# The up projection of seven products: sums of three token blocks made under the output projection, the last block's rows out of the load ring, down's first tiles moved

## The chip, the cores and the metric

The kernel runs on one core of one Trainium2 chip. Its time is the device time of one execution, in microseconds. The kernel before takes 2249.46 us (median of three runs, 2248.82 to 2249.55).

The engines of a core take their instructions in order, each from its own queue, and wait for one another by semaphores: TensorE (PE; PEld is its weight load), VectorE (DVE), ScalarE (ACT), GpSimd (POOL), and SyncE (SP), which here only issues DMA transfers.

## The reference

One layer of a streaming encoder for 1024 tokens of width 1024: two mixers, a merge, an output projection, then a gated MLP with a causal convolution of three taps. The change touches the path from the output projection on, all in float32:

```
x   = x + gate1 * (mix @ w_o)                                # 1024 x 1024
h2  = rms_norm(x, norm2_w) * (1 + scale2) + shift2
up  = h2 @ ffn_w_up                                          # 1024 x 5632
a, v = up[..., :2816], up[..., 2816:]
a   = gelu(causal_dwconv(a, ffn_conv_w, ffn_conv_b))
x   = x + gate2 * ((a * v) @ ffn_w_down)                     # 2816 x 1024
```

## The kernel before, in words

**Tiles and stages.** The tokens are 8 blocks of 128, the width of the MLP 22 tiles f of 128 columns. A float32 product is made of three passes: each operand is split into a high part (a cast on ScalarE, L143) and a low part (the rest, a subtraction on VectorE, L151), and hi x hi, hi x lo and lo x hi are summed in a PSUM bank. TensorE's matmuls come from one helper (L63), its transposes from L66; GpSimd's sums of two tiles are `gtt` (L139), its scalings `gmul` (L136).

**Output projection** (`wo`, up to L1566). For each block, four column quarters of 24 matmuls of 128 x 256 each; VectorE adds each result to the residual (L1537). `norm2` then squares a finished block (ScalarE, L1580), makes the root mean square (VectorE L1582, GpSimd L203) and scales the rows (GpSimd L136). `norm2_out` transposes the rows (tiles x2t), and ScalarE copies them out with scale and shift (L1602), the two halves of the width apart.

**Up projection in seven products** (`ups`). The matrix product of 2 x 2 blocks (token halves by halves of the width, against a and v columns) is made with seven products P1 to P7 instead of eight. Their token sides are B11, B21 (blocks 0 to 3, two halves of the width), B22 (second half of the width of blocks 4 to 7), and four combinations: T1 = f1 - B11, T2 = f2 - T1, T3 = f2 - f1, T4 = B21 - T2, where f1 and f2 are the halves of a block b of 4 to 7. Before, T1 is made in `norm2_out`; T2 is made there as a sum and split later by `late`, T3 too, and the sums of T4 (two on GpSimd for each block: L1631, and one through L139) are made by `late`, for blocks 4 to 7 in a row, when the pass "p5" begins. The weight sides are sums of the a and v columns of tile f, made by GpSimd in `prep` from raw tiles that `raw_w` loads (L1468, wa.. and wv..) into a ring "wr" of three tiles; the finished halves lie in a ring "w" of six (wP). `prep` runs LA = 5 products ahead. Each product is 12 matmuls of 128 x 512. Tiles 0 to 3 go in three passes: "pre" (P1 and P2, which need blocks 0 to 3 only), "p5" (P5), "rest" (P6, P7, P3, P4); tiles 4 to 21 go as "all" seven. After P3 ScalarE, VectorE and ScalarE make convolution and gelu of tile f (acc), after P4 GpSimd multiplies it by v (L139) and SyncE stores it (L1726).

**Down projection** (`downs`, `fetch`). 44 steps (22 tiles by two column halves), each 8 blocks of 3 matmuls. A step loads the gated tile (gr) and the weights (wdr), GpSimd scales the weights by the gate, and both are split (gh, gl, wd). Step 0 uses the rings of the up projection; the other steps use a ring of 16 tiles, laid over the memory that the combinations leave. `fetch` runs two steps ahead.

**What sets the order.** A planner (PEOrder) fixes TensorE's order: generators offer work with due times and ranks, as in `yield ((("xn", b),) + ..., 5.0)`: not before mark xn of block b plus 5 us of matmul time. The other engines take the program order as their scheduler arranges it. Memory is given out by pools: a tile laid over an older one waits until the last reader of that one is done.

Of the kernel before, what the change touches and what calls it, by code (L numbers as in the profile page):

```python
# [114 lines left out]
def _body(tc, nc, ctx, A, out):  # L115
# [1454 lines left out]
    last_sum = []  # L1570

    def norm2():
        for b in range(NB):
            yield ((("x1", b),) + ((("h2", b - 2),) if b >= 2 else ()), 0.0)
            if b < HB2 or b == NB - 1:
                xn = pw.tile([P, D], F32, tag="wr", bufs=3, name=f"xn{b}")
            else:
                xn = x_tile(f"xn{b}")
# [5 lines left out]
            gmul(xn, x1[b], rb)  # L1584
            xns[b] = xn
# [5 lines left out]
    def norm2_out():  # L1591
        for b in range(NB):
            yield ((("xn", b),) + ((("wo", 0),) if b == 0 else (("h2", b - 1),)), 7.0 if b in (0, NB - 1) else 5.0)
            xn = xns[b]
# [1 line left out]
            f = xn.rearrange("p (k c) -> p k c", c=P)
            f1, f2 = f[:, 0:4, :], f[:, 4:8, :]
            for k4 in (0, 4):
# [1 line left out]
                transposes(t, [xn[:, k * P:(k + 1) * P] for k in range(k4, k4 + 4)])  # L1600
                for k in range(k4, k4 + 4):
                    nc.scalar.activation(xn[:, k * P:(k + 1) * P], t[:, (k - k4) * P:(k - k4 + 1) * P], AF.Identity,  # L1602
# [213 lines left out]
```

## Time and profile before

| | us |
|---|---|
| median of three runs | 2249.46 |
| lowest, highest | 2248.82, 2249.55 |
| the profiled execution, its own time | 2251.65 |
| span of the profiled execution | 2249.9 |
| TensorE busy in the span (93.8%) | 2109.9 |
| VectorE, ScalarE, GpSimd busy | 1369.0, 902.5, 843.9 |

The mean granted clock of TensorE in that execution is 0.973 of full speed. A row of the timeline has a start and a duration in us, the engine, the line of the kernel, the operation with its output and inputs, the shape, how many instructions are drawn together, and in brackets the idle time of the engine ahead of it and the operation or transfer that ended it. PE rows overlap, since matmuls are pipelined.

### The profile page before, as it was taken

The page shows a single profiled execution, that of the slowest core. Times are in us where ns is not written, and L with a number is a line of the kernel's source. Part 1 is how long each engine was busy: PE and PEld are TensorE (multiplying, and loading weights), DVE is VectorE, ACT ScalarE, POOL GpSimd, SP SyncE. Part 2 cuts the span into 40 slices and gives each one's busy share as a digit, 9 for nine tenths or more (in the row PEclk, how much of TensorE's full clock was granted, in tenths as well). Part 3 has the DMA queues.
Part 4 walks back from the last instruction along what each step waited for, and adds up shares of the span by engine and source line. Part 5 has one row for each costly group of instructions (what it writes and reads, how often), then busy time and mean ns, then how long its engine had stood idle before and what let it go on. Part 6 is the DMA issues. An engine that isn't in the chain of part 4 may idle for free.

```text
span 2249.9 us, 30778 instructions
## 1 busy us (share of the span) xinstructions
PE 2109.9 (94%) x11553; PEld 1815.7 (81%) x11553; DVE 1369.0 (61%) x2197; ACT 902.5 (40%) x1817; POOL 843.9 (38%) x603
## 2 busy tenths in 40 slices
PE   7887899999999999899999999998899999999999
PEld 6776787878878799888778888897678888878887
DVE  6779499654655536658548885625665555554433
ACT  4554422363454522336225663226343343333231
POOL 4246620131122313338447760313653444442221
PEclk7999899999999999999999999999999999999999
DMA  8345742424333327588654427423232222244644
GB/s 251 104 126 161 180 130 89 131 75 136 94 94 113 94 78 231 187 267 274 231 162 122 141 76 243 131 76 94 78 110 85 85 82 79 83 141 150 215 147 153
DMA packets 279430, 309.32 MB, mean 137 GB/s; under 512 B 38815, under 2 KB 220396, under 8 KB 279024
## 3 DMA queue, kind: packets, MB, share of 16 engines
q1 hardware_dynamic: 279280, 307.35, 44.1%
q8 instruction: 91, 1.49, 0.3%
q14 instruction: 59, 0.48, 0.1%
HBM read 223.63 MB, written 83.66 MB: 137 GB/s over the span
## 4 chain that ended last, share of the span: by engine, by line
PE 36%; DVE 5%; issue 4%; POOL 4%; DMA 2%; ACT 1%; POOLq 0%; SPq 0%; ACTq 0%; DVEq 0%
PE d L63 11%; PE wo L63 4%; PE yb L63 4%; PE mx L63 3%; PE my L63 3%; PE m L63 3%; PE s L63 2%; PE mz L63 2%; PE o L63 1%; PE ya L63 1%; PE pT L66 1%; DVE qst L1186 1%; POOL acc L139 1%; DVE PTl L1258 1%; ACT P L1234 1%
## 5 line engine op out<-in xcount | busy, mean ns | idle before, releaser
L63 PE MATMUL d<-wd,gh 128*128 128x512 f32 x704 | 217.9, 391 | 2.5 <-DVE wd L151 1.8
L63 PEld LDWEIGHTS d<-wd,gh 128*128 128x128 f32 x704 | 132.8, 189 | 30.8 <-DVE wd L151 2.1
L63 PE MATMUL d<-wd,gl 128*128 128x512 f32 x352 | 137.6, 391 | 0.6 <-DVE gl L151 0.6
L139 POOL TENSOR_TENSOR wdr<-wdr,gf 128x512 f32<-128x512 f32 x44 | 61.2, 1392 | 162.9 <-DMA wdr<-in_ffn_w_down 124.9
L151 DVE TENSOR_TENSOR wd<-wdr,wd 128x512 fp32r<-128x512 f32 x44 | 31.3, 712 | 107.7 <-ACT wd L143 107.6
L143 ACT CAST wd<-wdr 128x512 fp32r<-128x512 f32 x44 | 27.3, 620 | 147.0 <-POOL wdr L139 128.7
L63 PEld LDWEIGHTS d<-wd,gl 128*128 128x128 f32 x352 | 66.5, 189 | 14.7 <-DVE gl L151 1.0
L1234 ACT ACTIVATE P<-s,nm 128x512 f32<-128x512 f32 (+2 forms) x96 | 55.3, 582 | 53.2 <-DVE nm L1232 44.1
L614 DVE TENSOR_TENSOR lt<-X 128x62 f32<-128x62 f32 (+30 forms) x62 | 68.0, 1097 | 11.0 <-DMA X<-bd_d 8.9
L136 POOL TENSOR_SCALAR P<-P,sm 128x896 f32<-128x896 f32 (+4 forms) x64 | 50.4, 794 | 63.9 <-DVE nm L1232 16.5
L139 POOL TENSOR_TENSOR acc<-acc,vv 128x512 f32<-128x512 f32 x44 | 63.8, 1469 | 24.4 <-ACT acc L1720 24.4
L63 PE MATMUL mz<-T2h,wP 128*128 128x512 f32 x176 | 62.4, 417 | 11.1 <-ACT wP L143 9.9
L151 DVE TENSOR_TENSOR gl<-gr,gh 128x1024 fp32r<-128x1024 f32 x44 | 60.6, 1377 | 15.6 <-ACT gh L143 15.3
L63 PE MATMUL m<-B21h,wP 128*128 128x512 f32 x176 | 60.1, 402 | 4.6 <-ACT u L1697 4.6
L66 PE MATMUL pT<-ident,P 128*128 128x128 f32 x288 | 48.9, 279 | 13.4 <-DVE PTl L1258 10.0
L1257 ACT CAST PTh<-pT 128x512 fp32r<-128x512 f32 (+2 forms) x96 | 46.0, 484 | 37.2 <-PE pT L66 36.9
L1116 DVE SCALAR_TENSOR_TENSOR ada<-wada,sc,ada 128x1024 f32<-128x1024 f32 x28 | 41.2, 1471 | 32.1 <-DMA wada<-in_w_ada 32.0
L63 PE MATMUL m<-B11h,wP 128*128 128x512 f32 x176 | 58.4, 395 | 0.0
L63 PE MATMUL my<-T4h,wP 128*128 128x512 f32 x176 | 57.8, 389 | 0.2 <-DVE vv L1708 0.2
L63 PE MATMUL mx<-B22h,wP 128*128 128x512 f32 x176 | 57.8, 389 | 0.0
L63 PE MATMUL my<-T3h,wP 128*128 128x512 f32 x176 | 57.8, 389 | 0.0
L63 PE MATMUL mx<-T1h,wP 128*128 128x512 f32 x176 | 57.3, 389 | 0.0
(1436 smaller groups left out, 7460.1 us busy)
## 6 DMA issues: line engine op xcount, KB each, us to landing
gr<-gg_d SPq DMA_DIRECT2D x44, 512.0 KB
wada<-in_w_ada SPq DMA_DIRECT2D x32, 512.0 KB
gg_d<-acc SPq DMA_DIRECT2D x22, 512.0 KB
wdr<-in_ffn_w_down SPq DMA_DIRECT2D x44, 256.0 KB
x<-in_x SPq DMA_DIRECT2D x16, 512.0 KB
ad<-in_w_ada SPq DMA_DIRECT2D x16, 512.0 KB
sg_d<-gst SPq DMA_DIRECT2D x32, 256.0 KB
q_d<-qst SPq DMA_DIRECT2D x48, 128.0 KB
```

The costliest lines, as they stand in the source:

```text
L63: self._pin(self.nc.tensor.matmul(out, lhsT, rhs, start=start, stop=stop, skip_group_check=more), cost)
L66: self._pin(self.nc.tensor.transpose(out=out, in_=in_, identity=ident), 0.107)
L136: return nc.gpsimd.tensor_scalar(o, i, by, 0.0, op0=ALU.mult, op1=ALU.add)
L139: nc.gpsimd.tensor_tensor(o, a, b, op=op)
L143: nc.scalar.copy(hi, src)
L151: return nc.vector.tensor_tensor(lo, src, hi.bitcast(F32), op=ALU.subtract)
L614: nc.vector.tensor_tensor(tv, X[:, 0:k, k:k + 1].broadcast_to([P, k, n]), X[:, k:k + 1, k + 1:64].broadcast_to([P, k, n]), op=ALU.mult)
L1116: nc.vector.scalar_tensor_tensor(acc, raw, sc[:, k:k + 1], acc, op0=ALU.mult, op1=ALU.add)
L1186: (gtt if LOP & (4 if n == "kst" else 8) else nc.vector.tensor_tensor)(o[r], raw[r], d[n][r].bitcast(F32), op=ALU.subtract)
L1234: nc.scalar.activation(Pt[:, kc], o, AF.Exp, bias=nm[:, 0:1], accum_out=sm[:, b:b + 1])
L1257: nc.scalar.copy(dh, tv)
L1258: nc.vector.tensor_tensor(PTl[:, k0:k0 + n, u * P:(u + 1) * P], tv, dh.bitcast(F32), op=ALU.subtract)
```

## The change

In `prep` the sum s1 = v1 + v2 is kept for the passes "pre", "p5" and "all"; "rest" takes P6's weights as v2 - (a1 - v1) in place of s1 - a1, the same value with one sum fewer. In `norm2` the square of block 7 has a ring tile of its own (sq7), and its rows go to two half tiles of another ring. `norm2_out` makes T1, T2 and T4's sums for blocks 4 to 7 on the spot and keeps them (`late` is a table now); `put_late` splits them when the pools for the combinations are open: T2 and T4 first, then T3. `fetch` moves ahead of `ups`, which loads the gate at tile 19 and calls `fetch(0)` at the last tile's P5; the tiles of the later down steps are three fixed sets of five.

```
@@ prep
-                if "s1" not in d:
-                    d["s1"] = h_tile(f"s1_{f}{kind}", ring="s").rearrange("p (k c) -> p k c", c=P)
-                    gtt(d["s1"], v1_, v2_, ALU.add)
-                    if "ra" in d:
+                if "s3" not in d:
+                    d["s3"] = v1_
+                    if kind != "rest":
+                        d["s1"] = h_tile(f"s1_{f}{kind}", ring="s").rearrange("p (k c) -> p k c", c=P)
+                        gtt(d["s1"], v1_, v2_, ALU.add)
+                    if kind != "p5":
                         gtt(v1_, a1, v1_, ALU.subtract)
             if q == "P6":
-                gtt(a1, d["s1"], a1, ALU.subtract)
+                gtt(a1, v2_, v1_, ALU.subtract)
@@ norm2
-            if b < HB2 or b == NB - 1:
+            if b < HB2:
                 xn = pw.tile([P, D], F32, tag="wr", bufs=3, name=f"xn{b}")
+            elif b < NB - 1:
+                xn = x_tile(f"xn{b}")
             else:
-                xn = x_tile(f"xn{b}")
+                xn = pw.tile([P, D], F32, tag="wr", bufs=3, name=f"sq{b}")
...
-            gmul(xn, x1[b], rb)
-            xns[b] = xn
+            if b < NB - 1:
+                gmul(xn, x1[b], rb)
+                xns[b] = [xn[:, c] for c in HS]
+            else:
+                xns[b] = [h_tile(f"xn{b}_{hf}", ring="s") for hf in range(2)]
+                for c, x in zip(HS, xns[b]):
+                    gmul(x, x1[b][:, c], rb)
@@ norm2_out
-            yield ((("xn", b),) + ((("wo", 0),) if b == 0 else (("h2", b - 1),)), 7.0 if b in (0, NB - 1) else 5.0)
+            yield ((("xn", b),), 6.0)
+            if b:
+                yield ((("h2", b - 1),), 1.0)
+            else:
+                yield ((("wo", 0),), 0.0)
...
                 gtt(t1, t1, b11l, ALU.subtract)
+                gtt(f2, f2, t1, ALU.subtract)
                 put("T1", tk, t1)
-                last_sum.append(nc.gpsimd.tensor_tensor(f2, f2, t1, op=ALU.subtract))
+                gtt(t4, b21h, f2, ALU.subtract)
+                gtt(t4, t4, b21l, ALU.add)
+                late[b] = {"T2": f2, "T3": f1, "T4": t4}
             pe.mark("h2", b)
-    def late(b, *names):
...
-        if "T4" in names:
-            b21h, b21l = [m[:, :, tk].bitcast(F32) for m in hc["B21"]]
-            follow(nc.gpsimd.tensor_tensor(f2, b21h, f2, op=ALU.subtract), last_sum[-1], True)
-            gtt(f2, f2, b21l, ALU.add)
-            put("T4", tk, f2)
@@ pools
-    t_ctx.close()
...
-    combos(pcm, "T2", "T3", "T4")
+    def put_late(names, bs):
+        for n in names:
+            for b in bs:
+                put(n, slice(b % HB2 * P, (b % HB2 + 1) * P), late[b][n])
+    combos(pool("pcm", pcm_ctx, side="right"), "T2", "T4")
+    put_late(("T2", "T4"), range(HB2, NB - 1))
+    t_ctx.close()
+    combos(pool("pcn", pcm_ctx, side="right"), "T3")
+    put_late(("T3",), range(HB2, NB - 1))
@@ fetch
+        def piece(name, dt, tag):
+            if n == 0:
+                return pw.tile([P, D], dt, tag=tag, bufs=3 if tag == "wr" else WB, name=f"{name}{n}")
+            return late_["pd"].tile([P, D], dt, tag=f"{name}{n % 3}", bufs=1, name=f"{name}{n}")
...
+        nc.sync.dma_start(gr, g_d[f])
+        nc.sync.dma_start(wr, wdn[f * P:(f + 1) * P, HS[hf]])
+        split(gh, gl, gr)
+        gtt(wr, wr, late_["gf2"][:, HS[hf]], ALU.mult)
+        follows[n] = split(dh, dl, wr)
@@ ups
-        for b in range(HB2, NB - 1):
-            late(b, "T2", "T3")
...
-                late(NB - 1, "T2", "T3")
-                for b in range(HB2, NB):
-                    late(b, "T4")
+                put_late(("T2", "T3", "T4"), [NB - 1])
...
+            if f == NF - 3 and q == "P4":
+                late_["gf2"] = x_tile("gf2")
+                nc.sync.dma_start(late_["gf2"], gate_d[5].broadcast_to([P, D]))
+            if f == NF - 1 and q == "P5":
+                fetch(0)
@@ after ups
-    gf2 = x_tile("gf2")
-    nc.sync.dma_start(gf2, gate_d[5].broadcast_to([P, D]))
-    fetch(0)
```

What becomes of the order. On TensorE, at the end of the output projection, before: the last three matmuls of block 7 (wo3_7), then the transposes of blocks 4, 5 and 6 (x2t4 to x2t6, half by half), then the first product of the up projection (m0_0).

```order
L63 MATMUL wo3_7_14545<-wo3_4h_13779,mh1_7_12944 128x256
L63 MATMUL wo3_7_14545<-wo3_4l_13780,mh1_7_12944 128x256
L63 MATMUL wo3_7_14545<-wo3_4h_13779,ml1_7_12945 128x256
L66 MATMUL x2t4_4_14580<-ident_73,xn4_14371 128x128 x4
L66 MATMUL x2t5_0_14604<-ident_73,xn5_14489 128x128 x4
L66 MATMUL x2t5_4_14613<-ident_73,xn5_14489 128x128 x4
L66 MATMUL x2t6_0_14637<-ident_73,xn6_14598 128x128 x4
L66 MATMUL x2t6_4_14646<-ident_73,xn6_14598 128x128 x4
L63 MATMUL m0_0_14690<-B11h_13513,wP1_0_14528 128x512
```

The same place after: the second half of block 6's transposes stands among the matmuls of the last quarter of block 7.

```order
L63 MATMUL wo3_7_14620<-wo3_0h_13772,mh1_0_12930 128x256
L63 MATMUL wo3_7_14620<-wo3_0l_13773,mh1_0_12930 128x256
L63 MATMUL wo3_7_14620<-wo3_0h_13772,ml1_0_12931 128x256
L66 MATMUL x2t6_4_14624<-ident_73,xn6_14510 128x128 x4
L63 MATMUL wo3_7_14620<-wo3_0h_13772,mh1_1_12932 128x256
L63 MATMUL wo3_7_14620<-wo3_0l_13773,mh1_1_12932 128x256
```

The transposes of blocks 4 to 6 (six sets of four) now stand between the matmuls of blocks 5 to 7 of the output projection, and the up projection's first product follows the last of these.

On GpSimd, where the sums for T4 stand before (xn with B21h or B21l: T4 of blocks 4 to 7; s_0rest, wv0rest, wa0rest: weights of tile 0 in the pass "rest").

```order
L1631 TENSOR_TENSOR xn_14371<-B21h,xn_14371 128x512
L1631 TENSOR_TENSOR xn_14489<-B21h,xn_14489 128x512
L1631 TENSOR_TENSOR xn_14598<-B21h,xn_14598 128x512
L139 TENSOR_TENSOR xn_14371<-xn_14371,B21l 128x512
L139 TENSOR_TENSOR s_0rest<-wv0rest 128x512
L1631 TENSOR_TENSOR xn_14631<-B21h,xn_14631 128x512
L139 TENSOR_TENSOR xn_14489<-xn_14489,B21l 128x512
L139 TENSOR_TENSOR xn_14598<-xn_14598,B21l 128x512
L139 TENSOR_TENSOR wv0rest<-wa0rest,wv0rest 128x512
L139 TENSOR_TENSOR xn_14631<-xn_14631,B21l 128x512
L139 TENSOR_TENSOR wa0rest<-s_0rest,wa0rest 128x512
L139 TENSOR_TENSOR wa0rest<-wa0rest 128x512
```

The same place after, from the scaling of block 7's rows (xn_0 and xn_1) to tile 0's weights; t_7 are block 7's T1 and T4, s_0p to s_3p the weight sums of the pass "p5".

```order
L136 TENSOR_SCALAR xn_0_14705<-x_7_14504,ss_13518 128x512
L136 TENSOR_SCALAR xn_1_14706<-x_7_14504,ss_13518 128x512
L139 TENSOR_TENSOR s_0p_14776<-wv0p_14774 128x512
L139 TENSOR_TENSOR t_7_14802<-xn_0_14705,B11h 128x512
L139 TENSOR_TENSOR t_7_14802<-t_7_14802,B11l 128x512
L139 TENSOR_TENSOR xn_1_14706<-xn_1_14706,t_7_14802 128x512
L139 TENSOR_TENSOR t_7_14803<-B21h,xn_1_14706 128x512
L139 TENSOR_TENSOR s_1p_14820<-wv1p_14818 128x512
L139 TENSOR_TENSOR s_2p_14843<-wv2p_14841 128x512
L139 TENSOR_TENSOR s_3p_14863<-wv3p_14861 128x512
L139 TENSOR_TENSOR t_7_14803<-t_7_14803,B21l 128x512
L139 TENSOR_TENSOR wv0rest<-wa0rest,wv0rest 128x512
```

Between the last norm and tile 0's weights GpSimd has one block's sums left; those of blocks 4 to 6 stand ahead of the norms of blocks 5 to 7, and the sum s_0rest is gone.

On ScalarE at the end of the up projection, before: acc_17622 and acc_17739 are the tiles f = 20 and 21, wd and gh the casts of down's first steps.

```order
L1720 ACTIVATE acc_17622<-acc_17622,v_93 128x1024
L1699 COPY xb_17647<-m_21_17648 128x512
L1717 ACTIVATE acc_17739<-xb_17647,v_92 128x1024
L143 CAST wd_17764<-wdr_17762 128x512
L143 CAST gh_17765<-gr_17763 128x1024
L1720 ACTIVATE acc_17739<-acc_17739,v_93 128x1024
L143 CAST wd_17789<-wdr_17787 128x512
L143 CAST gh_17790<-gr_17788 128x1024
```

The same place after.

```order
L1762 ACTIVATE acc_17626<-acc_17626,v_93 128x1024
L143 CAST gh_17704<-gr_17702 128x1024
L143 CAST wd_17706<-wdr_17703 128x512
L1741 COPY xb_17651<-m_21_17652 128x512
L1759 ACTIVATE acc_17755<-xb_17651,v_92 128x1024
L1762 ACTIVATE acc_17755<-acc_17755,v_93 128x1024
L143 CAST gh_17792<-gr_17790 128x1024
L143 CAST wd_17794<-wdr_17791 128x512
```

Step 0's casts have moved ahead of the last tile's convolution; step 1's come behind its gelu, as before.

## Rows read from the trace of the kernel before

**Rows 1.** Stretches: span, then each engine's busy us (instructions), clock, DMA share, GB/s.

```profile
1494.90:1544.30 49.40, 49.40 (x418) 49.40 (x417) 15.27 (x32) 24.33 (x55) 7.72 (x9) 1.00 0.26 86
1544.30:1657.90 113.60, 92.36 (x365) 71.58 (x364) 76.96 (x80) 54.20 (x101) 75.49 (x52) 0.89 0.30 88
1657.90:2001.20 343.30, 343.05 (x1513) 283.54 (x1511) 195.65 (x248) 132.28 (x195) 142.12 (x107) 1.00 0.27 85
2001.20:2012.60 11.40, 8.27 (x29) 6.16 (x29) 9.26 (x9) 5.00 (x6) 5.47 (x3) 0.85 0.65 207
2012.60:2249.90 237.30, 233.38 (x1030) 192.99 (x1028) 94.72 (x99) 65.61 (x82) 56.38 (x41) 1.00 0.52 170
```

**Rows 2.** TensorE: start, us, operation, [idle before <- what ended it].

```profile
1549.23 0.63 PE L66 MATMUL x2t<-ident,xn 128*128 128x128 f32 x4 [1.87 <-POOL ss L203]
1551.06 1.11 PE L66 MATMUL x2t<-ident,xn 128*128 128x128 f32 x4 [1.20 <-ACT xn L1602]
...
1562.45 0.80 PE L63 MATMUL m<-B21h,wP 128*128 128x512 f32 x1 [3.72 <-ACT u L1697]
...
1600.42 0.80 PE L63 MATMUL mz<-T2h,wP 128*128 128x512 f32 x1 [4.23 <-ACT wP L143]
...
1612.01 0.52 PE L63 MATMUL mz<-T2h,wP 128*128 128x512 f32 x1 [3.07 <-ACT wP L143]
...
1639.72 0.79 PE L63 MATMUL mz<-T2h,wP 128*128 128x512 f32 x1 [2.05 <-ACT wP L143]
```

**Rows 3.** The same view of SyncE's queue: weight loads as issued.

```profile
1545.33 0.38 SPq L1468 DMA_DIRECT2D wa3pre<-in_ffn_w_up  x1
1564.35 0.38 SPq L1468 DMA_DIRECT2D wv0p<-in_ffn_w_up  x1
1569.93 0.37 SPq L1468 DMA_DIRECT2D wv1p<-in_ffn_w_up  x1
...
1600.30 0.37 SPq L1468 DMA_DIRECT2D wa1rest<-in_ffn_w_up  x1
```

**Rows 4.** Waits of SyncE's queue from 1536 to 1660: total us, times, longest.

```profile
SPq L1468 <- DVE T4l L151: 18.6, 1, 18.6
```

**Rows 5.** The timeline of GpSimd (POOL).

```profile
1545.33 1.27 POOL L139 TENSOR_TENSOR t<-xn,B11h 128x512 f32<-128x512 f32 x1 [9.29 <-ACT xn L1602]
...
1549.28 1.12 POOL L136 TENSOR_SCALAR xn<-x,ss 128x1024 f32<-128x1024 f32 x1
...
1568.29 1.61 POOL L139 TENSOR_TENSOR s_0p<-wv0p 128x512 f32<-128x512 f32 x1 [4.53 <-DMA wv0p<-in_ffn_w_up]
...
1582.89 5.12 POOL L1631 TENSOR_TENSOR xn<-B21h,xn 128x512 f32<-128x512 f32 x3
...
1599.80 1.61 POOL L139 TENSOR_TENSOR wa0rest<-wa0rest 128x512 f32<-128x512 f32 x1
...
1630.67 2.54 POOL L139 TENSOR_TENSOR acc<-acc,vv 128x512 f32<-128x512 f32 x2 [4.35 <-ACT acc L1720]
```

**Rows 6.** The timeline of VectorE (DVE).

```profile
1544.46 0.42 DVE L1537 TENSOR_TENSOR x<-x,wo 128x256 f32<-128x256 f32 x1 [1.89 <-PE wo L63]
...
1552.12 1.75 DVE L1614 TENSOR_TENSOR xn<-xn 128x512 f32<-128x512 f32 x1 [1.18 <-POOL t L139]
...
1557.78 0.68 DVE L1614 TENSOR_TENSOR xn<-xn 128x512 f32<-128x512 f32 x1
...
1619.76 0.69 DVE L1714 TENSOR_TENSOR xb<-u,mx 128x512 f32<-128x512 f32 x1 [1.33 <-DMA wa3rest<-in_ffn_w_up]
```

**Rows 7.** Start of the down projection, timeline of TensorE.

```profile
2004.34 0.50 PE L63 MATMUL d<-wd,gh 128*128 128x512 f32 x1 [1.75 <-DVE wd L151]
```

**Rows 8.** The same of SyncE's queue.

```profile
2001.13 0.32 SPq L1754 DMA_DIRECT2D gr<-gg_d  x1
```

**Rows 9.** The same of ScalarE (ACT).

```profile
2003.78 1.15 ACT L1720 ACTIVATE acc<-acc,v 128x1024 f32<-128x1024 f32 x1 [1.75 <-DVE acc L1719]
...
2005.34 1.04 ACT L143 CAST gh<-gr 128x1024 fp32r<-128x1024 f32 x1
```

More of the change, by code (lines that the diff above doesn't have):

```diff
@@ L1569, in _body @@
     xns = {}
-    last_sum = []
+    late = {}
     def norm2():
@@ L1592, in norm2_out @@
         for b in range(NB):
[L1593 to L1594 removed]
+            yield ((("xn", b),), 6.0)
[3 more added lines that the diff above has]
+                yield ((("wo", 0),), 0.0)
             tk = slice(b % HB2 * P, (b % HB2 + 1) * P)
[L1596 to L1598 removed]
+            f1, f2 = [x.rearrange("p (k c) -> p k c", c=P) for x in xns[b]]
+            for k4, f in ((0, f1), (4, f2)):
                 t = bank("tp", f"x2t{b}_{k4}")
[L1600 removed]
+                transposes(t, [f[:, k, :] for k in range(4)])
                 for k in range(k4, k4 + 4):
[L1602 removed]
+                    nc.scalar.activation(f[:, k - k4, :], t[:, (k - k4) * P:(k - k4 + 1) * P], AF.Identity,
                                          bias=modc[:, 3 * KT + k:3 * KT + k + 1], scale=ab2[:, k:k + 1])
@@ L1609, in norm2_out @@
                 b11h, b11l = [m[:, :, tk].bitcast(F32) for m in hc["B11"]]
-                t1 = (h_tile(f"t1_{b}", ring="s") if b == NB - 1 else pt.tile([P, 512], F32, tag="tt", bufs=2, name=f"t1_{b}"))
-                t1 = t1.rearrange("p (k c) -> p k c", c=P)
+                b21h, b21l = [m[:, :, tk].bitcast(F32) for m in hc["B21"]]
+                if b == NB - 1:
+                    t1, t4 = [h_tile(f"t{i}_{b}", ring="s") for i in (1, 4)]
+                else:
+                    t1 = pt.tile([P, 512], F32, tag="t1", bufs=1, name=f"t1_{b}")
+                    t4 = pt.tile([P, 512], F32, tag="t4", bufs=3, name=f"t4_{b}")
+                t1, t4 = [t.rearrange("p (k c) -> p k c", c=P) for t in (t1, t4)]
                 gtt(t1, f1, b11h, ALU.subtract)
@@ L1645, in _body, with fetch @@
     pe.run(("wo", 1), ("h2", NB - 2))
-    t_ctx.close()
     wo_ctx.close()
     pcm_ctx = ctx.enter_context(ExitStack())
-    pcm = pool("pcm", pcm_ctx, side="right")
-    combos(pcm, "T2", "T3", "T4")
-    g_d = dr.tile([NF, P, S], F32, name="gg_d")
+    def put_late(names, bs):
[7 more added lines that the diff above has]
+    put_late(("T3",), range(HB2, NB - 1))
+    g_d = dr.tile([NF, P, S], F32, name="gg_d")
+    steps = [(hf, f) for hf in range(2) for f in range(NF)]
+    got = {}
+    late_ = {}
+    def fetch(n):
+        if n >= len(steps) or n in got:
+            return
+        hf, f = steps[n]
+        def piece(name, dt, tag):
+            if n == 0:
+                return pw.tile([P, D], dt, tag=tag, bufs=3 if tag == "wr" else WB, name=f"{name}{n}")
+            return late_["pd"].tile([P, D], dt, tag=f"{name}{n % 3}", bufs=1, name=f"{name}{n}")
+        gr = piece("gr", F32, "wr")
+        wr = piece("wdr", F32, "wr")[:, 0:512]
+        gh, gl = [piece(f"g{m}", F32R, "w") for m in "hl"]
+        d2 = piece("wd", F32R, "w")
+        dh, dl = d2[:, 0:512], d2[:, 512:1024]
+        nc.sync.dma_start(gr, g_d[f])
[3 more added lines that the diff above has]
+        follows[n] = split(dh, dl, wr)
+        got[n] = gh, gl, dh, dl
+    follows = {}
     def ups():
@@ L1729, in ups @@
             yield
[L1732 to L1760 removed]
     pe.add(2, ups(), True)
     pe.run(("up", NF - 1))
[L1763 to L1765 removed]
     pcm_ctx.close()
     pb_ctx.close()
[L1768 removed]
+    late_["pd"] = pd = pool("pd", side="right")
     xr = [pd.tile([P, 512], F32, name=f"xr{b}") for b in range(NB)]
```

32 lines of the change are left out of this document (removed).

## The prediction

> **What bounds the kernel now.** I began with the table of stretches [rows 1]: it cuts the last 755 us at the end of the output projection, the start of tile f = 4 of the up projection, the end of up and the first tenth of a step pair of down. Three of the five rows leave TensorE nothing to gain: it is busy for 49.40 of 49.40 us under the output projection, for 343.05 of 343.30 in f = 4 to 21, for 233.38 of 237.30 in the rest of down, each at a granted clock of 1.00. The long row also gives the pitch: 343.30 us for 1513 recorded matmuls, 0.227 us each. The other two rows are where time lies. From 1544.30 to 1657.90 TensorE stands for 113.60 - 92.36 = 21.2 us, and its clock is 0.89, so another 0.11 x 113.60 = 12.5 us go at the lower of its two levels: 33.7 us in all, and 79.9 of needed work. At the start of down it is 3.1 us idle and 0.15 x 11.40 = 1.7 at the lower clock: 4.8. So 38.5 us is all that this change can reach with what it touches; the floor is 2249.5 - 38.5 = 2211.
>
> Next, TensorE's timeline [rows 2], for where it stands: two transposes of normalised rows (1.9 and 1.2 us), a product P2 that waits for its bank (3.7 us), then P6 of f = 0, 1 and 3 (4.2, 3.1 and 2.1 us), each for ScalarE's cast of weights. From 1544.3, 7 sets of transposes at about 0.5 (an estimate from the first two rows) and the 144 matmuls of the passes "pre" and "p5" make 3.5 + 32.7 us, so P6 of f = 0 was due at 1580.5; it came at 1600.42. Thus 19.9 of the 33.7 us are lost ahead of that point and 13.8 behind it.
>
> Then the engines that TensorE waits for. SyncE's queue [rows 3] issues a weight load at 1545.33 and the next only at 1564.35, 19 us later, and wa1rest at 1600.30; its list of waits [rows 4] has 18.6 us for one T4 split: the load stood behind the last block's rows, which lay in the load ring until T4 was made of them. GpSimd [rows 5] has 75.49 of the 113.60 us full [rows 1] and takes its sums in the order in which the program asks: t1 sums at 1545, s_0p only after the load (1568.29, 3.9 us after its issue), the T4 sums from 1582.89, and f = 0's last weight sum ends at 1601.4. Under the output projection it had worked for 7.72 of 49.40 us [rows 1].
>
> **The change part by part.** *The sums moved under the output projection.* For blocks 4, 5 and 6 five GpSimd sums each (two for T1, one for T2, two for T4), 15 in all, leave the stretch with 33.7 us of loss or stand at its very beginning no more. One takes 1.27 us alone and about 1.7 beside VectorE (5.12 for three) [rows 5]: 19 to 26 us of queue. They go where GpSimd had 41.7 us free, so they fit; TensorE there has work at every moment, and that work is the cover. The transposes that they need move with them, from behind the last matmul of the output projection to between its matmuls: the stops of 1.9 and 1.2 us, which waited on the row norms, go. What they cost there the trace of before does not show; from below it is nothing; from above, block 7's norm queues behind block 6's five sums (8.7 us at 1.75) and all of it shows at TensorE. Block 6's first transposes stand some 36 matmuls of 49.40 / 418 = 0.118 us [rows 1], 4.2 us, ahead of the projection's end; with about 1.5 us for the copies out of the bank (an estimate) its sums end 3.7 to 6 us behind the end, block 7's power and scaling (1.12 us for the scaling [rows 5], 1.7 with both, an estimate) at 5.4 to 7.7, and its transposes are due 33 matmuls of up, 7.5 us, behind it. I take a stop of 1 us. VectorE's additions to the residual, 0.42 us [rows 6], now stand behind splits of up to 1.75; what waits for one is the bank of a product of 24 matmuls or 2.8 us, with a second bank to go on in, so nothing for those.
>
> *The last block's rows out of the ring.* Its square keeps a ring tile for a moment, its rows lie elsewhere. The load wv0p no longer waits for them or for the early splits: after 1545.33 it can go as soon as a tile of "pre" is split, near 1550 instead of 1564.35, and wa1rest near 1570, not 1600.30 [rows 3]. Its 18.6 us of wait [rows 4] go. What is late next: GpSimd's order. It has t1, T2 and T4 of block 7 (5 sums), four s sums and the three sums of f = 0, 12 in place of 23 from 1555 on: 12 x 1.3 to 1.75 = 16 to 21 us, from about 1554: ready at 1570 to 1575, plus a cast and a subtraction, before 1580.5.
>
> *Four weight sums fewer.* Per f = 0 to 3 the "rest" pass sums three tiles instead of four: 4 x 1.3 = 5 us of GpSimd, each in the chain ahead of P6 of its f.
>
> *What remains of the 33.7.* Ahead of P6 of f = 0: 1 us for block 7's transposes and 1.5 at the lower clock behind that stop (four transposes that took 0.63 us at 1549.23 took 1.11 at 1551.06, behind two stops [rows 2]). So 19.9 - 2.5 = 17.4 gained. Behind it: P6 of f = 1 lost 3.1 us, to a load that now starts 30 us sooner; I leave 1.5, since its sums still follow those of f = 0 on GpSimd. P6 of f = 3 lost 2.1; GpSimd takes acc of f = 0 ahead of its sums, and that waits for the gelu: from xb at 1619.76 [rows 6] to acc at 1630.67 [rows 5] are 10.9 us, a chain that the change leaves alone; I leave 2.5, plus 0.5 for f = 2 and 2 for the clock. So 13.8 - 6.5 = 7.3. Together 24.7.
>
> *Down's first tiles.* Before, the second step's load could not start until up's last matmul had read T4 (it went at 2001.13 [rows 8]), and VectorE's and ScalarE's work on step 0 came behind the last tile's convolution: TensorE stood 1.75 us for wd [rows 7]. After, the first tiles are made while up's last products run, and the load for step 1 lies over T1, whose last reader is P5, 48 matmuls or 10.9 us sooner. ScalarE's gelu (1.15 us at 2003.78) still comes ahead of the second gh cast (1.04 at 2005.34 before) [rows 9], and the first bank is read by the last products: I leave 2.0 of the 4.8 us, bounds 0 and 4.8. Gain 2.8. The gate's load moves up beside the weight loads of f = 19, where the DMA engines are 0.27 busy [rows 1]: nothing, and up to one load of 3.9 us late for a weight tile without that room.
>
> *The sum.* 24.7 + 2.8 = 27.5. The profiled execution took 2251.65 us (span 2249.9 and 1.75 around it): 2224.2 by its time. The runs' median is 2.2 us lower: 2222.
>
> *A rule weighed.* VectorE's same subtraction took 0.68 us with GpSimd free (1557.78) and 1.75 with it at work (1552.12) [rows 6]; the 1.07 more is most of one GpSimd sum. The Trainium skill (SBUF — State Buffer, "Who interferes with whom") has it that a VectorE instruction with two operands in SBUF and a GpSimd instruction that reads SBUF shut each other out for the whole instruction. By that rule, which the two rows agree with, the sums moved under the output projection also wait for VectorE's splits there; if all five sums of block 6 took 1.7 instead of 1.27, block 7's norm would be 2.1 us later, and the time 2224; with VectorE mostly away, as under the projection before (15.27 of 49.40 us [rows 1]), it stays 2222, which I keep.
>
> **The rivals.**
> *A, the stall moves into the output projection.* GpSimd's 15 sums get in the way of the norms of blocks 5, 6 and 7, the transposes that now stand between the projection's matmuls stop everything behind them, and each stop is followed by the lower clock. For it: TensorE takes its instructions in order, and the norm's own chain (square, power, scaling 1.12 us [rows 5]) is behind those sums on one queue. Against it: 41.7 us free. Price: 3 stops of 3 us and 2 us of clock for each, 15; gain 12.5, time 2237.
>
> *B, only the first wait goes.* P6 of f = 0 comes in time, but f = 1 to 3 still lack weights, since loads of 3.9 us, three sums and the acc sums share one ring and one queue; the 13.8 us behind 1600 stay. For it: P6 of f = 3 waited though no T4 sum was near. Against it: a pair's chain, three sums of 1.3 and two loads, is about 12 us and runs ahead, against 48 matmuls or 10.9 us. Gain 17.4 + 2.8 = 20.2, time 2229.
>
> *C, slower: down's three sets.* Tiles of down were a ring of 16, now three fixed sets of five, so that the cast of wd for step n+3 may not start until TensorE has read all of step n (before, the ring gave it the place of an earlier gr). Chain from there: cast 0.62, subtraction 0.69, against two steps of 24 matmuls or 10.9 us until it is wanted. It decides only if the chain, with loads and the queue ahead of it, comes to more than that: if each of 43 steps lost 0.8 us, 34 us, the time would be 2257. Against it: gh stood under the same bond before, and all of down lost 237.3 - 43 x 24 x 0.227 = 3 us.
>
> *D, nothing moves.* The sums could stand elsewhere and the stops stay as they are, 2249. Against it: the order of the built program has them between the norms.
>
> **How the numbers follow.** Forecast (gain of 22 to 33, time 2217 to 2227) 0.58; B 0.18; A 0.13; C 0.04; D 0.03; the remaining 0.04 is a gain near the full 38.5. The range goes from the floor, 2211, to just beyond A, 2239. About 0.2% or 4.5 us is what a measurement of this kernel can tell from no change: forecast, A, B and the floor are faster, 0.93; D same, 0.03; C slower, 0.04.
>
> **What will show it.** The first matmul of f = 4 should come at about 1544.3 + 79.9 + 9 = 1633 on this trace's clock in place of 1657.9, the granted clock up to there above 0.93 and the idle time under 8 us; wv0p issued before 1552 and wa1rest before 1575; no wait of SyncE for a T4 split; P6 of f = 0 before 1584. The output projection should show GpSimd at 27 to 34 us and TensorE still full; stops above 2 us there mean A. Waits for P6 of f = 1 to 3 above 3 us each mean B. At down's start the two stops should sum to under 2 us; idle time spread over all steps of down means C. A stretch as long as before means that I misread what holds GpSimd's order.

## The result, and the profile after

The changed kernel takes 2228.26 us (median of 4 runs, 2217.35 to 2231.01) against 2249.14 (4 runs, 2248.34 to 2249.55): a ratio of 0.990, 95% interval 0.9865 to 0.9932, 20.9 us by the medians. The forecast was 2222, with a range of 2211 to 2239. The profiled execution took 2231.01 us (span 2229.3).

Two traces are best compared by landmarks, since the part ahead of the output projection, whose instructions the change leaves alone, ran 2.7 us longer in this one: the projection's first matmul stands at 1450.91, before at 1448.20. From there:

| us | before | after | won | forecast |
|---|---|---|---|---|
| first matmul of the output projection to first of f = 4 | 209.73 | 188.86 | 20.9 | 24.7 |
| first of f = 4 to first of down | 344.15 | 342.90 | 1.2 | |
| first of down to the end of the span | 247.82 | 246.63 | 1.2 | 2.8 with the row above |
| start to first matmul of the projection | 1448.20 | 1450.91 | -2.7 | 0 |

The stretches of the changed kernel, with the columns of [rows 1]; the first two are the output projection, the third reaches to f = 4, the fifth is the start of down:

```profile
1450.90:1497.60 46.70, 46.70 (x391) 46.69 (x390) 17.63 (x28) 10.09 (x13) 12.75 (x9) 1.00 0.23 79
1497.60:1550.40 52.80, 51.71 (x436) 51.51 (x436) 24.08 (x40) 35.65 (x83) 24.85 (x21) 1.00 0.27 91
1550.40:1639.70 89.30, 82.50 (x346) 66.66 (x345) 62.88 (x73) 43.72 (x73) 53.75 (x37) 0.94 0.38 112
1639.70:1982.50 342.80, 342.80 (x1514) 283.63 (x1513) 198.53 (x250) 132.99 (x196) 142.48 (x107) 1.00 0.28 90
1982.50:1994.00 11.50, 9.66 (x42) 7.35 (x41) 9.28 (x7) 5.14 (x7) 7.44 (x4) 1.00 0.39 105
1994.00:2229.30 235.30, 230.93 (x1018) 190.56 (x1016) 115.46 (x99) 63.35 (x81) 62.19 (x40) 1.00 0.53 168
```

The reader sees the third row, which answers to the second of [rows 1]: 89.30 us in place of 113.60, GpSimd 53.75 us full in place of 75.49, and a clock of 0.94 in place of 0.89. TensorE still stands for 6.8 us there, and 0.06 x 89.30 = 5.4 us are lost to the lower clock. The projection now has idle time (1.1 us), GpSimd works 24.85 us under its second half, and up runs without a stop. The stops that remain, in TensorE's timeline:

```profile
1545.19 0.66 PE L66 MATMUL x2t<-ident,xn 128*128 128x128 f32 x4 [1.09 <-POOL xn L136]
...
1561.01 1.12 PE L66 MATMUL x2t<-ident,xn 128*128 128x128 f32 x4 [3.59 <-POOL xn L136]
```

```profile
1597.08 0.73 PE L63 MATMUL mz<-T2h,wP 128*128 128x512 f32 x2 [0.35 <-DVE wP L151]
...
1621.32 0.50 PE L63 MATMUL mz<-T2h,wP 128*128 128x512 f32 x1 [2.51 <-ACT wP L143]
```

The stops of [rows 2] ahead of P6 of f = 0 and of f = 1 and for the bank of P2 are gone (0.35 us are left within P6 of f = 1). A stop of 3.59 us for block 7's norm has come, with transposes at the lower clock behind it (1.12 us for four), and that for f = 3 has stayed (2.51; before 2.05). SyncE's queue, against [rows 3]:

```profile
1552.19 0.38 SPq L1468 DMA_DIRECT2D wa3pre<-in_ffn_w_up  x1
1554.07 0.38 SPq L1468 DMA_DIRECT2D wv0p<-in_ffn_w_up  x1
...
1579.08 0.37 SPq L1468 DMA_DIRECT2D wa1rest<-in_ffn_w_up  x1
1588.24 0.37 SPq L1468 DMA_DIRECT2D wv1rest<-in_ffn_w_up  x1
```

wv0p goes 1.9 us after wa3pre (before 19), and what is left of waits for a T4 split is 0.3 us; but wv1rest follows wa1rest only after 9 us. At down's start the stops of 0.75, 1.75 and 0.63 us come to 0.54, 1.30 and 0.42, the last two now in steps 1 and 2 (the third, at 1996.79, is not shown):

```profile
1984.05 0.73 PE L63 MATMUL d<-wd,gh 128*128 128x512 f32 x2 [0.54 <-DVE vv L1765]
...
1990.63 0.50 PE L63 MATMUL d<-wd,gh 128*128 128x512 f32 x1 [1.30 <-DVE wd L151]
```

### The profile page after: what moved, and what is told of

Same layout as the page of the kernel before. It is cut to its first block, busy times and chain, and to the rows that moved or that the text cites. A ratio compares the mean times of both kernels' runs of the same rounds, so it can differ in the third digit from the quotient of the medians.

```text
span 2229.3 us, 30774 instructions
## 1 busy us (share of the span) xinstructions
PE 2103.6 (94%) x11553; PEld 1814.4 (81%) x11553; DVE 1387.3 (62%) x2197; ACT 901.6 (40%) x1817; POOL 848.3 (38%) x600
## 4 chain that ended last, share of the span: by engine, by line
PE 41%; DVE 4%; DMA 2%; POOL 2%; issue 1%; ACT 1%; POOLq 0%; SPq 0%; ACTq 0%; DVEq 0%
PE d L63 11%; PE m L63 5%; PE my L63 5%; PE mx L63 5%; PE yb L63 4%; PE wo L63 4%; PE s L63 3%; PE mz L63 2%; PE o L63 1%; PE ya L63 1%; PE pT L66 1%; DVE qst L1186 1%; DVE PTl L1258 1%; ACT P L1234 1%; DVE nm L1227 1%
## 5 line engine op out<-in xcount | busy, mean ns | idle before, releaser
L139 POOL TENSOR_TENSOR wdr<-wdr,gf 128x512 f32<-128x512 f32 x44 | 68.7, 1564 | 163.5 <-DMA wdr<-in_ffn_w_down 148.1
L143 ACT CAST gh<-gr 128x1024 fp32r<-128x1024 f32 x44 | 46.1, 1050 | 153.6 <-PE d L63 153.1
L151 DVE TENSOR_TENSOR wd<-wdr,wd 128x512 fp32r<-128x512 f32 x44 | 61.2, 1392 | 1.2 <-ACT wd L143 1.2
```

What stands on the lines that cost most here:

```text
L139: nc.gpsimd.tensor_tensor(o, a, b, op=op)
L143: nc.scalar.copy(hi, src)
L151: return nc.vector.tensor_tensor(lo, src, hi.bitcast(F32), op=ALU.subtract)
```

## The experiments

The time of one execution spreads by more than some of these effects, so each kernel is also read by the stretch from the projection's first matmul to the first of f = 4 in its profile, called the stretch below. The changed kernel run twice gave 188.86 and 189.22 there, before and before with down's edits 209.73 and 209.84: in these two pairs it repeats to 0.4 us. Inside it less is fixed: P6 of f = 0 came 139.8 us after the projection's start in the first profile of the changed kernel and 138.5 in the second. Each stretch is read from one profile; each ratio is to the kernel before in the same batch, whose median lay between 2249.14 and 2252.13.

| kernel | stretch, us | median, us | ratio to before (95%) |
|---|---|---|---|
| before | 209.73 | 2249.14 to 2252.13 | 1 |
| before + weight sums | 207.30 | 2251.14 | 1.0005 (0.9992 to 1.0018) |
| before + rows out of the ring | 205.87 | 2246.26 | 0.9982 (0.9970 to 0.9995) |
| before + due times | 196.05 | 2236.18 | 0.9928 (0.9915 to 0.9942) |
| before + down's edits | 209.84 | 2246.50 | 0.9975 (0.9963 to 0.9988) |
| changed | 188.86 | 2228.26 | 0.9899 (0.9865 to 0.9932) |
| changed, again | 189.22 | 2230.99 | 0.9917 (0.9894 to 0.9940) |
| changed - due times | 201.26 | 2240.86 | 0.9963 (0.9951 to 0.9976) |
| changed - T4 moved | 188.53 | 2225.69 | 0.9897 (0.9882 to 0.9912) |
| changed - rows out of the ring | 189.48 | 2227.75 | 0.9910 (0.9887 to 0.9933) |
| changed + norm first | 191.54 | 2229.44 | 0.9909 (0.9888 to 0.9930) |
| changed + norm first + v tiles | 183.95 | 2221.16 | 0.9887 (0.9861 to 0.9914) |
| changed + v tiles | 182.09 | 2220.23 | 0.9859 (0.9845 to 0.9872) |
| changed + norm first + v tiles + T3 later | 181.35 | 2218.38 | 0.9845 (0.9832 to 0.9859) |

**The changed kernel again.** No edit.

> The changed kernel once more, to learn how far its executions spread and where. Its first profile is 20.6 us shorter than that of before: 23.3 us won from the output projection on, 2.7 us lost ahead of it, in a part whose instructions are the same. If those 2.7 us are chance of that one execution, the first matmul of the output projection comes near 1448 us this time (1448.2 before, 1450.9 after) and the median near 2226. Rival: the change itself makes the part ahead slower; then it is near 1451 again and the median stays at 2228 to 2229.

The projection began at 1452.23, later still, and the median was 2230.99. But in the other profiles of this study it begins anywhere from 1443.13 to 1450.12, with most of the change in as with little of it (1443.13 for the changed kernel without the due times, 1444.70 without T4's move, 1450.12 for before with the weight sums). So 2.7 us lie within the spread between executions, and both expectations, which hung on one number, asked too much of it. Chance is not shown, though: the two profiles of the changed kernel itself are the latest two of the 14. What the part ahead of the projection adds is left out from here on.

**Due times alone, on the kernel before.**

```
-            yield ((("xn", b),) + ((("wo", 0),) if b == 0 else (("h2", b - 1),)), 7.0 if b in (0, NB - 1) else 5.0)
+            yield ((("xn", b),), 6.0)
+            if b:
+                yield ((("h2", b - 1),), 1.0)
+            else:
+                yield ((("wo", 0),), 0.0)
```

> The kernel before with the planner's due times of the transposes alone as changed (blocks 4 to 6 between the matmuls of the output projection), T4's sums, ring, weight sums and down as before. From the first matmul of the output projection to the first of f = 4 before takes 209.7 us. Theory of the prediction: the four stops at the transposes (4.3 us) and the clock behind them go, the held loads stay: 202 to 206. Rival: the ring frees earlier as well, since block 7's norm is no later, and most of the 20.9 us comes from here: under 198. Other rival: nothing, the stops move into the projection: 208 to 211.

196.05: 13.7 us, two thirds of the whole, beyond the theory and at the rival. GpSimd and TensorE of this kernel:

```profile
1567.88 5.13 POOL L1635 TENSOR_TENSOR xn<-B21h,xn 128x512 f32<-128x512 f32 x3
...
1587.05 1.28 POOL L139 TENSOR_TENSOR wa0rest<-wa0rest 128x512 f32<-128x512 f32 x1
```

```profile
1587.67 0.79 PE L63 MATMUL mz<-T2h,wP 128*128 128x512 f32 x1 [5.98 <-ACT wP L143]
...
1598.91 0.79 PE L63 MATMUL mz<-T2h,wP 128*128 128x512 f32 x1 [3.58 <-ACT wP L143]
```

T4's sums still stand in a row, but start 121.1 us after the projection's first matmul (1567.88 - 1446.81) against 134.7 before, because nine sums for T1 and T2 of blocks 4 to 6 come with the transposes, the first eight of them before the projection has ended, with no other edit. P6 of f = 0 still waits 5.98 us, yet comes 140.9 us after the projection's start instead of 152.2. The four stops at the transposes (4.3 us before) are gone as well; the edit moves both, and no run parts them.

**All parts but the due times.** The edit above, taken back in the changed kernel.

> The changed kernel with the planner's due times of the transposes as before; all other parts as changed (so all sums are still made with the transposes, but these stand behind the output projection again). Theory now: the place of the transposes carries the gain; alone on the kernel before it gave 13.7 of 20.9 us. Then the stretch from the first matmul of the output projection to f = 4 is 200 to 206 us (188.9 with it, 209.7 before). Rival, the prediction's: ring, moved T4 sums and fewer weight sums each give their own, and 193 to 197 remain.

201.26, as the theory had it. All 15 sums are back behind the projection, and TensorE stops there as before, on the banks' copies and on weights:

```profile
1555.20 0.50 PE L63 MATMUL m<-B21h,wP 128*128 128x512 f32 x1 [1.61 <-ACT u L1735]
...
1568.43 0.50 PE L63 MATMUL m<-B11h,wP 128*128 128x512 f32 x1 [3.71 <-ACT xa L1737]
...
1588.58 1.22 PE L63 MATMUL mx<-T1h,wP 128*128 128x512 f32 x2 [4.17 <-DVE wP L151]
```

**T4's sums back at the pass p5, all else as changed.**

```
-                gtt(t4, b21h, f2, ALU.subtract)
-                gtt(t4, t4, b21l, ALU.add)
-                late[b] = {"T2": f2, "T3": f1, "T4": t4}
+                late[b] = {"T2": f2, "T3": f1, "T4": f2}
...
-                put_late(("T2", "T3", "T4"), [NB - 1])
+                put_late(("T2", "T3"), [NB - 1])
+                put_late(("T4",), range(HB2, NB))
```

> The changed kernel with T4's eight sums made in a row at the pass p5 as before, all else as changed. Theory: on the kernel before, with the transposes early, P6 of f = 0 still waited 5.98 us behind T4's eight sums on GpSimd (1567.9 to 1582.3); so without the move it waits 3 to 6 us again, the clock falls behind it, and the stretch is 193 to 197 us against 188.9. Rival: with the earlier loads and without the extra sum they fit ahead of P6 (block 7's norm gets through sooner too, since block 6's T4 sums no longer stand ahead of it): 187 to 190.

188.53: the theory fell. Making T4 early is worth nothing here, though it is the part that took the worst wait of the trace before away. TensorE's stops say why:

```profile
1550.04 0.66 PE L66 MATMUL x2t<-ident,xn 128*128 128x128 f32 x4 [0.18 <-POOL xn L136]
...
1590.30 0.80 PE L63 MATMUL mz<-T2h,wP 128*128 128x512 f32 x1 [4.93 <-ACT wP L143]
```

Without T4's sums ahead of it block 7's norm is in time (0.18 us in place of 3.59), and P6 of f = 0 begins without a stop; P6 of f = 1 waits 4.93 us. The two prices are nearly the same.

**The rows out of the ring, alone and taken back.** These lines, with the halves read in place of xn where it is used; in the changed kernel they are undone.

```
+                xn = pw.tile([P, D], F32, tag="wr", bufs=3, name=f"sq{b}")
...
+                xns[b] = [h_tile(f"xn{b}_{hf}", ring="s") for hf in range(2)]
+                for c, x in zip(HS, xns[b]):
+                    gmul(x, x1[b][:, c], rb)
```

> The kernel before with one edit, the last block's rows out of the load ring. Theory of the prediction: the load of wa1rest held for 18.6 us by T4's split goes early, wv0p too, and the stretch falls from 209.7 to 201 to 206 us. Rival: taken back into the ring in the changed kernel they cost 0.5 us only (189.5 against 188.9 and 189.2), so the ring is not what binds: 208 to 210.

> The changed kernel with the last block's rows in the load ring again, all else as changed. Theory of the prediction: the ring holds the loads up. Then wv0p is still early, but the load two places on waits for the T3 and T2 splits of block 7 (about 1574), wa1rest goes 5 to 10 us later than 1579, and the time is 3 to 8 us more. Rival: with T4 made elsewhere the rows leave the ring soon enough and the loads are bound by the ring's other tiles anyway; then within 1 us.

Alone it gives 3.9 us, just inside the theory; taken back it costs 0.3 to 0.6, the rival of that run. SyncE's queue of the first:

```profile
1544.46 0.38 SPq L1468 DMA_DIRECT2D wv0p<-in_ffn_w_up  x1
...
1572.79 0.37 SPq L1468 DMA_DIRECT2D wa1rest<-in_ffn_w_up  x1
1597.24 0.37 SPq L1468 DMA_DIRECT2D wv1rest<-in_ffn_w_up  x1
```

wa1rest goes at 1572.79 (in [rows 3] 1600.30), but the next load behind it in the ring waits until 1597.24, when the first sums of the pass rest are split: the hold moved by one load, and P6 of f = 1 waited 4.59 us. With the sums done earlier, T2's split frees the rows soon enough: the ring with the rows in it held a load for 8.3 us, with no loss behind it. Either edit, the rows out of the ring or T4's sums made early, takes the long hold away: with the due times alone wa1rest waits for T4's split and goes 137.7 us after the projection's start; in the changed kernel it goes at 128.2, with the rows back in the ring at 129.4, with T4's sums back at p5 at 117.5. So taking one of the two back cannot price it.

**Four weight sums fewer, alone.**

```
+                    if kind != "rest":
...
-                gtt(a1, d["s1"], a1, ALU.subtract)
+                gtt(a1, v2_, v1_, ALU.subtract)
```

> The kernel before with one edit, four weight sums fewer on GpSimd in the pass rest. Theory: one sum of 1.3 us lies ahead of P6 in each of f = 0 to 3, so the stops of 4.2, 3.1, 0.5 and 2.1 us shrink by up to 1.3 each, with less of the lower clock behind them: 204 to 207 us for the stretch against 209.7. Rival: the loads set the pace, and it moves under 1 us.

207.30, 2.4 us, 0.3 short of the theory's range; the time does not show it (ratio 1.0005, 0.9992 to 1.0018, at best 1.8 us). The stop for f = 0 shrank from 4.2 to 1.3, for f = 3 from 2.1 to 1.4, while f = 1 went from 3.1 to 4.7, bound by its load at 1603.28.

**Down's edits alone, on the kernel before.** The new `fetch`, with

```
+            if f == NF - 3 and q == "P4":
+                late_["gf2"] = x_tile("gf2")
...
+            if f == NF - 1 and q == "P5":
+                fetch(0)
```

> The kernel before with down's edits alone (the gate's load and step 0 inside the up projection, three sets of tiles). From the first matmul of f = 4 to the end of the span before takes 592.0 us, after 589.5. Theory: 2 to 3 us less than before here (589 to 590), the stretch ahead of it at 209 to 210, and down's steps at the same pace, 44 steps in 246 to 247 us. Rival of the prediction: the three sets cost a little in each step; then the start gains 2 to 3 us and the steps lose as much, 592.

1655.30 to 2244.8 are 589.5 us in place of 592.0: 2.5, and 246.68 from the first matmul of down, as after (246.63). The three sets cost nothing.

**Block 7's norm first.** In the changed kernel T4's sums of block 6 follow its scaling on GpSimd; the splits of T2 and T4 of blocks 4 to 6 follow its mean square:

```
+        follow(nc.gpsimd.tensor_tensor(t4, b21h, f2, op=ALU.subtract), scaled[-1], True)
+        gtt(t4, t4, b21l, ALU.add)
...
+                    follow(nc.scalar.copy(hi, late[b][n]), ms[NB - 1])
```

> The changed kernel with block 7's norm put first: T4's two sums of block 6 follow its scaling on GpSimd, and the splits of T2 and T4 of blocks 4 to 6 follow its mean square on VectorE. Theory: the stop of 3.59 us ahead of block 7's transposes comes from these being queued ahead (the mean square ran at 1557.93 though the square was done at 1554.05, and the power took its turn behind two sums that end at 1556.2). Then the stop falls below 1 us, the lower clock behind it goes, and the time is 4 to 6 us less than that of the changed kernel. Rival: the norm's own chain sets it; then less than 1 us changes, or the sums come back as a wait for P6 of f = 0 and nothing is won.

191.54: 2.5 us worse in the stretch, which neither had (the median, 2229.44, does not tell it from the changed kernel). The stop ahead of the transposes went, as the theory said, and a new one came, but not where the rival looked. TensorE, then ScalarE:

```profile
1554.38 0.60 PE L66 MATMUL x2t<-ident,xn 128*128 128x128 f32 x4
...
1566.31 0.50 PE L63 MATMUL m<-B11h,wP 128*128 128x512 f32 x1 [4.01 <-ACT xa L1754]
```

```profile
1562.20 1.66 ACT L1665 CAST T3h<-xn 128x512 fp32r<-128x512 f32 x3 [2.66 <-DVE T4l L1666]
1563.76 1.50 ACT L1614 ACTIVATE xn<-x2t,modc,ab 128x128 f32<-128x128 f32 x4
1565.14 0.62 ACT L1767 COPY xb<-xa 128x512 f32<-128x512 f32 x1
1565.65 0.60 ACT L1754 COPY xa<-m 128x512 f32<-128x512 f32 x1
```

The transposes come without a stop, 7.7 us after the end of the projection (1546.69 to 1554.38); but the T3 casts, whose tiles lie over the tile that T4's split of block 6 still reads, stand 2.66 us at the head of ScalarE's queue, and the copy that frees P2's bank (xa, 1565.65) behind them: 4.01 us.

**The v tiles in another ring,** with the norm first and without it:

```
-        r = pw.tile([P, KT, P], F32, tag="wr", bufs=3, name=f"w{'av'[v]}{f}{tag}")
+        if tag == "rest" and v == 1:
+            r = x_tile(f"wv{f}{tag}").rearrange("p (k c) -> p k c", c=P)
+        else:
+            r = pw.tile([P, KT, P], F32, tag="wr", bufs=3, name=f"w{'av'[v]}{f}{tag}")
```

> The one with block 7's norm first, and the raw v tiles of the pass rest (tiles 0 to 3) loaded into the ring of six that holds xb and acc, not the load ring of three. Theory: GpSimd's waits of 6.0, 6.7 and 7.3 us for the loads of f = 1, 2 and 3 come from the ring of three, and P6 of f = 3 waits 2.5 us because the sums stand behind acc of f = 0. Then the loads go 10 us sooner, GpSimd takes the sums of f = 3 ahead of acc, and the stops for P6 of f = 1 to 3 (3.2 us together with 2.4 of clock) go: 4 to 6 us less than the kernel with the norm first alone. Rival: TensorE was bound there by the cast and subtraction, or the acc tiles now wait; then under 1 us.

> The changed kernel with one edit, the raw v tiles of the pass rest loaded into the ring of six instead of the load ring. Theory: the 5.4 us that went between P6 of f = 0 and f = 4 (49.1 us for 192 matmuls at 0.227, 43.5) are the ring of three alone: 43.5 to 44, the stretch from the output projection's first matmul to f = 4 183 to 184 us, and the stop of 3.6 us ahead of block 7's transposes unchanged. Rival: it needed the earlier norm as well; then 186 to 189.

Both by the theory and a little beyond it: 183.95, 7.6 less than with the norm first (4 to 6 expected), and 182.09 for the edit alone (183 to 184). From P6 of f = 0 to f = 4 43.8 us are left of 49.1, without a stop. That part, in the columns of [rows 1], and GpSimd there, both of the edit alone:

```profile
1583.47:1627.29 43.82, 43.78 (x193) 35.98 (x192) 39.19 (x44) 21.13 (x30) 23.71 (x16) 1.00 0.27 85
```

```profile
1597.12 1.77 POOL L139 TENSOR_TENSOR wv3rest<-wa3rest,wv3rest 128x512 f32<-128x512 f32 x1 [9.62 <-DMA wv3rest<-in_ffn_w_up]
...
1600.68 2.15 POOL L139 TENSOR_TENSOR wa3rest<-wa3rest 128x512 f32<-128x512 f32 x1
1604.28 2.99 POOL L139 TENSOR_TENSOR acc<-acc,vv 128x512 f32<-128x512 f32 x2 [1.45 <-ACT acc L1765]
```

GpSimd now takes the sums of f = 3 (to 1602.8) ahead of acc. Behind the projection this edit leaves only the stop for block 7's norm (in it, the 1.1 us stay):

```profile
1555.28 1.11 PE L66 MATMUL x2t<-ident,xn 128*128 128x128 f32 x4 [3.59 <-POOL xn L136]
```

**And the T3 casts behind block 7's copies.** `follow(c, casts[0], True)` on the T3 casts of blocks 4 to 6, casts[0] being block 7's B22 cast.

> Norm of block 7 first, raw v tiles of the pass rest in the ring of six, and the T3 splits of blocks 4 to 6 behind block 7's B22 cast on ScalarE. Theory: with the norm first the stop did not go, it moved: ScalarE stood 2.66 us for T4's split of block 6 (the T3 tiles lie over the tile it reads), ahead of the copy that frees the bank of P2, and TensorE stood 4.01 us. With the T3 casts behind that copy the stop goes. From the first matmul of the output projection to the first of f = 4: 178 to 180 us, against 183.95 with the T3 casts where they were and 188.9 for the changed kernel; median 2214 to 2217. Rival: the next wait (block 7's own sums for P5, or T4's split) takes its place; then 182 to 184.

181.35: between theory and rival. The stop of 4.01 is gone; four of 0.55 to 0.93 us are there, two of them for ScalarE's copies of u (4.1 us in all with the 1.12 in the projection). It is the fastest kernel here, by medians 9.9 us ahead of the changed one, but it is ahead of the v tiles alone by 0.7 us of the stretch only, which the runs don't tell apart.

## Why the prediction was right, and where its steps were off

**The sign and the size.** 23.3 us are won from the projection on, 27.5 were forecast; the median lies in the range. What bounds: right. Of the 33.7 us named as within reach ahead of f = 4 the changed kernel takes 20.9, with the v tiles 27.6 (182.09, against 176.0 with no loss). Ahead of P6 of f = 0, 17.4 were forecast and 12.5 came (13.7 in the second profile); behind it 7.3 were forecast and 8.4 came (6.8). The sum was built on how much loss would be left, not on what each edit gives, so its size could come right without the cause.

**Where it came from: wrong in part.** The prediction gave the gain ahead of P6 of f = 0 to three parts together, the moved sums, the ring and four sums fewer, with a price for none, and named the ring's 18.6 us of wait and T4's sums as the cause. The runs show the main carrier, the transposes' place on TensorE: 13.7 us alone, 12.2 when taken away last (201.26 - 189.0). It brings nine sums under the projection; T4's six are not needed there (188.53 without). The other 7.0 us (196.05 - 189.0) come from the ring, T4's sums and the weight sums together. The ring is worth 3.9 alone and 0.4 when taken back, T4's move nothing when taken back, the weight sums 2.4 alone; these were never taken back from the changed kernel, and the ring and T4's move, which each free the load, were never taken back together. How the 7.0 us divide stays open. The 18.6 us of [rows 4] were the wait of wa1rest; the 19 us ahead of wv0p were a wait for a split of weights, which [rows 4] leaves out.

**The mis-sized term** is the stop for block 7's transposes, 1 us and 1.5 of clock behind it. It was 3.59, plus 1.1 in the projection where nothing was set, and behind it the granted clock was 0.50 from 1560.3 to 1567.1, some 3.4 us more: 8.1 in place of 2.5, which covers the 5 us missing ahead of P6 of f = 0. VectorE and GpSimd of the changed kernel:

```profile
1553.32 3.48 DVE L151 TENSOR_TENSOR T2l<-xn,T2h 128x512 fp32r<-128x512 f32 x2
1556.72 1.28 DVE L151 TENSOR_TENSOR T4l<-t,T4h 128x512 fp32r<-128x512 f32 x2
1557.93 0.14 DVE L1586 TENSOR_SCALAR ss<-ss 128x1 f32<-128x1 f32 x1
1557.99 0.68 DVE L151 TENSOR_TENSOR T2l<-xn,T2h 128x512 fp32r<-128x512 f32 x1
1558.59 0.68 DVE L151 TENSOR_TENSOR T4l<-t,T4h 128x512 fp32r<-128x512 f32 x1
1559.19 0.68 DVE L151 TENSOR_TENSOR wP<-wa3pre,wP 128x512 fp32r<-128x512 f32 x1
1559.79 0.68 DVE L151 TENSOR_TENSOR wP<-wa2pre,wP 128x512 fp32r<-128x512 f32 x1
```

```profile
1554.63 1.62 POOL L139 TENSOR_TENSOR t<-t,B21l 128x512 f32<-128x512 f32 x1
1558.15 0.93 POOL L203 TENSOR_TENSOR ss<-ss,mhalf 128x1 f32<-128x1 f32 x1 [1.89 <-DVE ss L1586]
1559.18 3.39 POOL L136 TENSOR_SCALAR xn<-x,ss 128x512 f32<-128x512 f32 x2
...
1592.45 1.29 POOL L139 TENSOR_TENSOR wv1rest<-wa1rest,wv1rest 128x512 f32<-128x512 f32 x1 [5.99 <-DMA wv1rest<-in_ffn_w_up]
...
1614.52 2.55 POOL L139 TENSOR_TENSOR acc<-acc,vv 128x512 f32<-128x512 f32 x2 [7.34 <-DMA wv3rest<-in_ffn_w_up]
```

GpSimd's sums for block 6 end at 1556.25, 5.7 us behind the projection's end, inside the 3.7 to 6 of the prediction. From there two things went otherwise. The mean square ran at 1557.93, behind the splits of T2 and T4 that VectorE had been given (1.89 us for GpSimd): this queue the prediction did not look at. The power took 0.93 us (0.54 before), and the scaling 3.39 for two halves, against 1.12 for the whole in [rows 5], beside VectorE's splits; without the due times, where VectorE had one split there, the two halves took 1.79. The prediction had "VectorE mostly away"; in these rows it works without a pause. Without the wait, and with power and first half at 0.54 and 0.56 us, the rows would have come at 1557.4, just when the transposes were due (1561.01 - 3.59): 1.9 us of the stop are the mean square's, the rest the slower GpSimd. The run with the norm first bears this out: with those splits behind the mean square and T4's sums behind the scaling, the stop went. The rule of the Trainium skill that was weighed there (SBUF — State Buffer, "Who interferes with whom") speaks of GpSimd instructions that read SBUF, and scaling and power are such: with its price on the norm, not on the sums alone, it would have given nearly half of the 3.59 us. The trace agrees with it, as far as two rows side by side can. (Of the prediction's own two rows, the one at 1557.78 was not wholly beside a free GpSimd: a sum began 0.23 us into it, and took 1.58.)

**Behind P6 of f = 0** 6.5 us were left and about 5.5 measured (7.1 in the second profile), but for f = 1 to 3 the loads set the pace, with GpSimd's order behind them: GpSimd waited 5.99 us for wv1rest (row above) and 6.7 for wv2rest, and wv3rest landed only with the gelu of f = 0 (1614.5), so that acc went ahead. The v tiles in another ring took all of it. Rival B had the mechanism, at the wrong price.

**Down:** 2.8 forecast, 2.4 measured, half of it ahead of down's first matmul.

**The rivals.** A had the right place, since block 7's norm behind the sums is its mechanism, at a third of its price. C and D fell: down from its first matmul is 1.2 us shorter, and the sums moved. (C's terms, 27.5 gained and 34 lost, make 2256 and not 2257.)

**The marks.** From the projection's start P6 of f = 0 was to come before 135.8 us and came at 139.8, wa1rest before 126.8 and at 128.2, f = 4 at 184.8 and came at 188.9. wv0p (103.8 and 103.2), the clock (0.93 and 0.94) and the idle time (8 and 6.8 us) met theirs, and no P6 waited 3 us. GpSimd was to be busy 27 to 34 us under the projection; that counted from the 7.72 us of [rows 1], whose row is the projection's second half. There it was 24.85, since 12 of the 15 sums fell into it: 17 us more, against 19 to 26 forecast. TensorE had one stop of 1.1 us.

## What to carry to other kernels

When several edits aim at one wait, ask which one moves the work that stands first in the queue; the others may only shorten a wait that the first has already taken off the path. For an instruction that must be on time, follow each engine of its chain and what stands ahead of it there, the short step (here a mean square of 0.14 us on VectorE) as well as the long one. Before making a load earlier, count which tile of its ring it takes and when the last reader of that tile is done: another ring for one of two operands was worth more than the earlier issue.

## What the runs showed of the hardware

Executions of one program spread: before took 2239.76 to 2258.54 us in the 11 runs beside the second run of the changed kernel, with a mean granted clock of 0.980 in the shortest and 0.970 in the longest, and 2248.34 to 2249.55 in its first four. The part ahead of the projection, the same instructions in all 14 profiles, took from 1443.1 to 1452.2 us. What sets it in one execution these runs don't show. A scaling of 128 x 512 on GpSimd took 1.7 us beside VectorE's splits of two operands (3.39 for two), where 128 x 1024 had taken 1.12 and, with the rows back in the ring, took 2.20 beside the same splits.
